# Feed-forward opening of a hybrid decoder trunk: three products of the two opened gate pairs in narrow form, and steps of the weight sums issued earlier

## The chip, the cores and the metric

The kernel runs on one core of a Trainium2 chip. A core has TensorE (PE, with its weight loads shown as PEld), VectorE (DVE), ScalarE (ACT), GpSimd (POOL) and SyncE (SP), which run side by side, each through its own queue in order, and 16 DMA engines that serve the queues of SP, ACT and POOL. Products are accumulated in PSUM, in banks of 128 x 512 float32. The metric is the device time of one execution in microseconds.

## The reference

Two decoder layers over 512 tokens of width 1024, in float32: the first mixes tokens by a gated short convolution, the second by sliding-window attention with sinks. Each is followed by the same feed-forward, with 2816 hidden channels, which is where the change lies:

```python
def swiglu(h, w_gate_up, w_down):
    g, u = jnp.split(h @ w_gate_up, 2, axis=-1)
    return (jax.nn.silu(g) * u) @ w_down

for l in range(DEPTH):
    ...
    ff = swiglu(rmsnorm(h, ffn_pre_norm[l]), ffn_w_gate_up[l], ffn_w_down[l])
    h = h + rmsnorm(ff, ffn_post_norm[l])
```

## The kernel before

**Precision.** Every operand is split into a high part (rounded by ScalarE, L504) and a low part (the rest, by VectorE, L505). A product is three matmuls: high by low, high by high, low by high (`mm3`, L209 to L212).

**Seven products.** The hidden channels are taken in 22 blocks of 128. The first two (PLAIN) are computed directly, as four plain tiles (`plain_job`, L1411; gate and up of each). The other 20 make ten pairs of blocks q = 0 to 9. For a pair, weights and tokens are cut into halves and the product is formed by a scheme of seven products instead of eight, numbered 1 to 7 (`gate_jobs`, L1218). Each product multiplies one sum of weight blocks with one sum of token blocks (`factors`), for e = 0 and 1 (gate and up) and four steps k. The results share PSUM: chain X takes products 1, 6, 7, 4 one on top of the other, Z takes 5 (and 3), Y takes 2. After each product `take` (L1243) adds the state of the chain to tiles in SBUF: `st`, `u` and `gr`, whose halves are g0 and g1. Because 6, 7 and 4 go on in the bank that the takes read, the matmuls of the next product of X wait for the take of the last one.

**Broad and narrow.** A broad chain (L1310 to L1316) has two banks, one for each e. A matmul 512 wide multiplies the high weights with high and low tokens side by side, so the two halves of a bank hold two parts of one sum, and a second matmul 256 wide adds the low weights. The take must add both halves of both banks: four operations on 128 x 256. A narrow chain (L1318 to L1321) has one bank: its halves are e = 0 and 1, and each k takes three matmuls of 256. One operation on 128 x 512 adds all of it. Here X is broad for all pairs, Z also from q = 3 on.

**Opened pairs.** For q = 0 and 1 (OPENED) products 1 and 2 are computed earlier, in narrow form, while the layer before ends (`Opening`, L1196). What is left are 6, 5, 7, 3, 4, with takes of their own (`early`, L1252 to L1267).

**Order.** A feed-forward is one list of jobs (`in_line`, L509): four plain tiles; five products of pair 0; five of pair 1; seven of pair 2; eleven jobs of the first down product (accumulated by L676); pair 3 and so on. When job j has run, job j + 3 (LINE_LEAD) is prepared: L504 and L505 split its weights, sometimes after L492 has added two weight tiles. Then one of the late parts of an earlier pair is run (L616 to L628). PE, VectorE, ScalarE and POOL keep this written order. Weights come through seven raw tiles on SP's queue (L471), each fetched when one is free.

**Sums of weights.** Other sums of weight blocks are made in HBM by POOL's DMAs, some of them accumulating (L575). `sum_on` (L595) first issues whatever is still left in a list, then puts the next step of each sum in progress on it. After every job, a few of the list are issued, each waiting for the split of the weights three jobs on (L539); behind a plain tile that has no such split they do not wait. The names at which a step is taken are in a table (BEGIN); "o1" and "0f0" (in layer 1 "1f0") are taken after the first plain tile, "0f1" (or "1f1") after the second.

Of the kernel before, what the change touches and what calls it, by code (L numbers as in the profile page):

```python
# [26 lines left out]
OPENED = 2  # L27
# [58 lines left out]
def yoco_kernel(  # L86
# [389 lines left out]
    class Job:  # L476
# [10 lines left out]
        def add(self):  # L487
            if callable(self.make):
                self.make()
            elif self.make:  # L490
                raw = self.raws[0].tile
                nc.vector.tensor_tensor(out=raw, in0=raw, in1=self.raws[1].tile, op=ALU.add)  # L492
# [92 lines left out]
    for l in range(2):  # L585
# [3 lines left out]
        for rd, (f0, f1) in enumerate(ROUNDS[:-1]):  # L589
            k = slice(f0 // 2, f1 // 2)  # L590
# [4 lines left out]
    def sum_on(at, behind=None):  # L595

        issue(len(issues), behind)
        if at in BEGIN:
            summing.append(sums_of[BEGIN[at]])
        for x in summing:  # L600
            x.step()
        summing[:] = [x for x in summing if x.steps]
# [169 lines left out]
    for k in range(KT):  # L772
# [11 lines left out]
        for n in range(9):  # L784
            i, t = (n % 3, n // 3) if k == 0 else (n // 3, n % 3)
            n = 3 * k + t
# [45 lines left out]
    both = []  # L832
# [342 lines left out]
    def ffn(l, before, ahead, gain, gpres, following):  # L1175
# [42 lines left out]
        def gate_jobs(q, factors, out, to, then):  # L1218

            sums = sums_of[f"g{l}{q}"]
            a21, a22, a11, a12 = (Raw(b) for b in sums.blocks)
            s1, s3, *rest = (Raw(b) for b in sums.sums)
            raws = {1: [a11], 2: [a12], 5: [s1], 7: [s3], 4: [a22]}
            if rest:
                raws[6], raws[3] = ([r] for r in rest)
            else:
                raws[6], raws[3] = [a11, s1], [a12, a11]
            five = q >= FIVE  # L1230
            broad = "XZ" if five else "X"
            chain = {1: "X", 6: "X", 7: "X", 4: "X", 5: "Z", 3: "V" if five else "Z", 2: "Y"}
            pools = {"X": ps_mm, "Y": ps_pt, "V": ps_pt, "Z": ps_sc}
            if q == 0:

                pools = {"X": ps_sc, "Y": ps_pt, "V": ps_pt, "Z": ps_mm}
            banks, kept = {}, []
            early = opened_pairs[q] if q < OPENED else None

            def tiles(a):  # L1240
                return a.rearrange("p (e c) -> p e c", e=2)

            def take(p):  # L1243
                x, y, z, v = (banks.get(c) for c in "XYZV")
                st, u, gr = kept[:3]
                g0, g1 = (gr.rearrange("p (e h c) -> p e h c", e=2, h=2)[:, :, h]
                          for h in range(2))

                def add(out, a, b):
                    nc.vector.tensor_tensor(out=out, in0=a, in1=b, op=ALU.add)  # L1250

                if early and p == 6:  # L1252
                    both = slot("st")
                    kept.append(both)
                    for e in range(2):
                        c = slice(e * 256, (e + 1) * 256)
                        add(both[:, c], x[e][:, :256], st[:, c])
                        add(both[:, c], x[e][:, 256:], both[:, c])
                elif early and p == 5:
                    add(u, z, st)  # L1260
                elif early and p == 3:
                    add(g1, tiles(z), tiles(kept[3]))
                elif early and p == 4:
                    for e in range(2):
                        c = slice(e * 256, (e + 1) * 256)
                        add(st[:, c], x[e][:, :256], st[:, c])
                        add(st[:, c], x[e][:, 256:], st[:, c])  # L1267
                elif p == 2:
                    add(g0, tiles(y), tiles(st))
                elif p == 5:  # L1270
                    if not five:
                        nc.scalar.activation(u, z, AF.Copy)
                        return
                    for e in range(2):
                        ue = u[:, e * 256 : (e + 1) * 256]
                        nc.scalar.activation(ue, z[e][:, :256], AF.Copy)
                        add(ue, z[e][:, 256:], ue)
                    add(st, u, st)
                elif p == 3:
                    add(g1, tiles(v if five else z), tiles(st))  # L1280
                else:
                    for e in range(2):
                        a, b = x[e][:, :256], x[e][:, 256:]
                        ste, ue = (v[:, e * 256 : (e + 1) * 256] for v in (st, u))
                        if p == 7:
                            add(ue, a, ue)
                            add(ue, b, ue)
                            continue
                        nc.scalar.activation(ste, a, AF.Copy)  # L1289
                        add(ste, b, ste)  # L1290
                if p == 4:
                    for g, m in ((g0, st), (g1, u)):
                        nc.vector.scalar_tensor_tensor(out=g, in0=tiles(m), scalar=-1.0, in1=g,
                                                       op0=ALU.mult, op1=ALU.mult)

            def run(p):
                def products(job):
                    if not kept:
                        kept.extend([early.st, slot("st"), early.gr] if early
                                    else [slot("st"), slot("st"), wide("gr")])  # L1300
                    whi, wlo = job.w
                    c = chain[p]
                    opened = c not in banks
                    if opened:
                        banks[c] = ([bank("g" + c.lower(), pools[c]) for _ in range(2)]
                                    if c in broad else bank("g" + c.lower(), pools[c]))
                    steps = [(e, k, slice(e * S + k * P, e * S + (k + 1) * P))
                             for e in range(2) for k in range(4)]
                    kw = {"skip_group_check": True}
                    if c in broad:  # L1310
                        for e, k, kk in steps:
                            nc.tensor.matmul(banks[c][e], whi[:, kk], factors[p][k][2],  # L1312
                                             start=opened and k == 0, stop=False, **kw)
                        for e, k, kk in steps:
                            nc.tensor.matmul(banks[c][e][:, :256], wlo[:, kk], factors[p][k][0],  # L1315
                                             start=False, stop=k == 3 and p in (4, 5), **kw)  # L1316
                    else:
                        for e, k, kk in steps:  # L1318
                            mm3(banks[c][:, e * 256 : (e + 1) * 256], whi[:, kk], wlo[:, kk],
                                *factors[p][k][:2], opened and e == k == 0,  # L1320
                                e == 1 and k == 3 and p in (2, 3), **kw)  # L1321
                    take(p)
                return products

            def gate():
                nc.scalar.activation(kept[2], kept[2], AF.Silu)  # L1326

            def end():
                late = out(kept[2], to)
                then()  # L1330
                return late

            return [Job(raws[p], run(p), {3: gate, 4: end}.get(p), len(raws[p]) > 1)
                    for p in (1, 2, 6, 5, 7, 3, 4)[2 if early else 0 :]]
# [41 lines left out]
        with tc.manual_schedule(engines=ALL):  # L1376
# [34 lines left out]
            def plain_job(n):  # L1411
                def run(job):
                    pss.append(bank("pgu", ps_mm))
                    project(pss[n], ahead.ready[2 * OPENED + n], xs)

                def then():
                    if n == 0:
                        if l == 0:
                            sum_on("o1")
                        sum_on(f"{l}f0")  # L1420
                    if n == 1:
                        sum_on(f"{l}f1")
                    return gate_pair(*pss[n - 1 :]) if n % 2 else None

                return Job([], run, then)
# [5 lines left out]
            for rd, (f0, f1) in enumerate(ROUNDS):  # L1431
                last = rd == len(ROUNDS) - 1
                for f in range(max(f0, PLAIN), f1, 2):
                    q = (f - PLAIN) // 2
# [10 lines left out]
            n = f1 - f0  # L1445
# [6 lines left out]
            for at, job in zip(LAST, closing):  # L1452
                job.slots = True
                jobs.insert(len(jobs) - at, job)
            in_line(jobs, late)
            if l == 1:
                nc.gpsimd.drain()
# [281 lines left out]
    early = [Early(u) for u in range(2 * NB)]  # L1739
    at = []  # L1740

    with tc.manual_schedule(engines=ALL):
# [20 lines left out]
        for hf in range(2):  # L1763
            c = slice(hf * 256, (hf + 1) * 256)
# [63 lines left out]
    with tc.manual_schedule(engines=ALL):  # L1828
        sum_on("a0")
        for i in range(KT + 2):  # L1830
# [9 lines left out]
            for c in order.split():  # L1840
# [23 lines left out]
                op, n = c[0], [int(d) for d in c[1:].rstrip("-")]  # L1864
                t = i - late
                if op == "g":

                    u = 2 * (t - EARLY - 1) + n[0]
# [128 lines left out]
```

## Time and profile before

| | us |
|---|---|
| median of 3 runs (lowest, highest) | 1018.8 (1018.78, 1019.55) |
| the profiled execution | 1019.24 |
| its span, first to last instruction | 1017.5 |
| PE busy | 999.8 |
| VectorE busy | 914.6 |
| ScalarE busy | 603.1 |
| POOL busy | 184.5 |

All times below count from the start of the span. Layer 0's opened pairs run from 211 to 243, layer 1's from 711 to 743.

A timeline row gives start, duration, engine, line, operation, tiles (out<-in), shape and how many such instructions were merged; in brackets, how long the engine stood idle before it and what ended that. Merged rows span all their instructions. Matmuls overlap, so PE's pace is read from start to start, not from durations. A row of waits gives total, number and longest. A row by stretches gives the window, its length, the busy time of PE, PEld, DVE, ACT and POOL (with instructions), then the granted TensorE clock as a share of full speed, the share of DMA time in use, and GB/s.

### The profile page before, as it was taken

What the parts mean: (1) busy time and instruction counts of PE and PEld (TensorE: products, weight loads), DVE (VectorE), ACT (ScalarE), POOL (GpSimd) and SP (SyncE); (2) the same over time, 40 slices, a digit from 0 to 9 for tenths busy, and PEclk for the clock granted to TensorE, in tenths of its full rate; (3) what the DMA queues carried; (4) which work ended last, traced back from release to release, by engine and by line L of the source; (5) the groups of instructions that cost most, each with busy time, mean ns of one, the idle gap of its engine ahead of it and who ended that gap; (6) DMA issues with size and microseconds to landing.
All of it is one profiled execution on the core that took longest, in us unless ns stands there. A gap on an engine that the chain in (4) does not pass through costs nothing. (4 is left out here: it accounts for less than half of the span.)

```text
span 1017.5 us, 16125 instructions
## 1 busy us (share of the span) xinstructions
PE 999.8 (98%) x5848; PEld 879.5 (86%) x5848; DVE 914.6 (90%) x1572; ACT 603.1 (59%) x1085; POOL 184.5 (18%) x250
## 2 busy tenths in 40 slices
PE   9999999998999999999999999999999999999997
PEld 7899888988889898898898888898888888989986
DVE  7899877899789999999878998878997999999996
ACT  8445545754656465566485788778446664645641
POOL 0211022112101011000022756420211010110001
PEclk9999999999999999999999999999999999999999
DMA  9886987678969789769504889965999576979742
GB/s 339 269 246 205 336 260 275 222 234 248 328 238 284 257 285 307 240 216 341 203 1 134 219 242 254 284 230 142 343 299 322 171 246 223 290 277 276 241 166 83
DMA packets 68447, 248.69 MB, mean 244 GB/s; under 512 B 8080, under 2 KB 8848, under 8 KB 56592
## 3 DMA queue, kind: packets, MB, share of 16 engines
q1 hardware_dynamic: 53200, 150.24, 39.7%
q0 software_dynamic: 14592, 96.48, 37.0%
q8 instruction: 46, 0.75, 0.3%
q10 hardware_dynamic: 576, 0.95, 0.2%
q14 instruction: 33, 0.27, 0.1%
HBM read 241.34 MB, written 102.76 MB: 338 GB/s over the span
## 5 line engine op out<-in xcount | busy, mean ns | idle before, releaser
L505 DVE TENSOR_TENSOR wlo<-raw,whi 128x1024 fp32r<-128x1024 f32 (+1 forms) x227 | 274.2, 1213 | 26.1 <-ACT whi L504 26.0
L504 ACT ACTIVATE whi<-raw 128x1024 fp32r<-128x1024 f32 (+1 forms) x227 | 234.8, 1050 | 103.8 <-DVE raw L492 59.1
L1312 PE MATMUL gx<-xt,whi 128*128 128x512 f32 x480 | 122.5, 398 | 6.9 <-DVE st L1250 6.9
L1312 PEld LDWEIGHTS gx<-xt,whi 128*128 128x128 f32 x480 | 87.3, 191 | 24.0 <-ACT whi L504 4.7
L575 POOL DMA_DIRECT2D hsum<-in_w_gb_dram x96 | 63.5, 722 | 156.5 <-ACT whi L504 109.9
L575 POOL DMA_DIRECT2D hsum<-hsum x32 | 25.3, 790 | 355.7 <-ACT whi L504 296.0
L1250 DVE TENSOR_TENSOR st<-gx,st 128x256 f32<-128x256 f32 x208 | 81.2, 418 | 4.7 <-PE gx L1315 2.0
L1315 PEld LDWEIGHTS gx<-xt,wlo 128*128 128x128 f32 x480 | 65.6, 191 | 4.8
L1315 PE MATMUL gx<-xt,wlo 128*128 128x256 f32 x480 | 66.9, 282 | 0.0
L1289 ACT ACTIVATE st<-gx 128x256 f32<-128x256 f32 x96 | 34.7, 380 | 50.6 <-PE gx L1315 41.6
L1326 ACT ACTIVATE gr<-gr 128x1024 f32<-128x1024 f32 x20 | 21.2, 1062 | 61.2 <-DVE gr L1250 61.2
L210 PE MATMUL px<-wlo,ahi 128*128 128x512 f32 x120 | 46.8, 390 | 1.5 <-DVE mix L676 1.5
L212 PE MATMUL px<-whi,alo 128*128 128x512 f32 x120 | 46.7, 389 | 0.0
L211 PE MATMUL px<-whi,ahi 128*128 128x512 f32 x120 | 46.7, 389 | 0.0
L575 POOL DMA_DIRECT2D hsum<-in_w_dn_dram x48 | 31.9, 765 | 80.3 <-ACT whi L504 64.2
L210 PE MATMUL gy<-xlo,whi 128*128 128x256 f32 x144 | 40.8, 283 | 0.0
L211 PE MATMUL gy<-xhi,whi 128*128 128x256 f32 x144 | 40.8, 283 | 0.0
L212 PE MATMUL gy<-xhi,wlo 128*128 128x256 f32 x144 | 40.7, 283 | 0.0
L676 DVE TENSOR_TENSOR mix<-mix,px 128x512 f32<-128x512 f32 x54 | 34.7, 679 | 1.5 <-PE px L212 1.5
L320 POOL TENSOR_TENSOR ur<-uv,mhalf 128x1 f32<-128x1 f32 x15 | 13.9, 928 | 113.7 <-DVE uv L315 113.6
L492 DVE TENSOR_TENSOR raw<-raw,raw 128x1024 f32<-128x1024 f32 x28 | 34.1, 1219 | 0.1
L442 ACT ACTIVATE whi<-raw 128x1024 fp32r<-128x1024 f32 x18 | 19.3, 1082 | 23.6 <-DMA raw<-in_w_gb_dram 7.9
(367 smaller groups left out, 3062.4 us busy)
## 6 DMA issues: line engine op xcount, KB each, us to landing
hsum<-in_w_gb_dram POOLq DMA_DIRECT2D x96, 512.0 KB, 7.9
raw<-hsum SPq DMA_DIRECT2D x88, 512.0 KB, 7.6
raw<-in_w_gb_dram SPq DMA_DIRECT2D x64, 512.0 KB, 6.7
hsum<-in_w_dn_dram POOLq DMA_DIRECT2D x36, 512.0 KB, 8.2
raw<-in_w_dn_dram SPq DMA_DIRECT2D x32, 512.0 KB, 6.6
hsum<-hsum POOLq DMA_DIRECT2D x28, 512.0 KB, 6.1
hsum<-in_w_dn_dram POOLq DMA_DIRECT2D x12, 768.0 KB, 13.6
raw<-in_w_in_dram SPq DMA_DIRECT2D x13, 512.0 KB, 6.9
```

Of the source, the lines that this page charges most:

```text
L210: nc.tensor.matmul(out, whi, xlo, start=start, stop=False, **kw)
L211: nc.tensor.matmul(out, whi, xhi, start=False, stop=False, **kw)
L212: nc.tensor.matmul(out, wlo, xhi, start=False, stop=stop, **kw)
L492: nc.vector.tensor_tensor(out=raw, in0=raw, in1=self.raws[1].tile, op=ALU.add)
L504: self.begun = nc.scalar.activation(hi[:, :n], raw, AF.Copy)
L505: nc.vector.tensor_tensor(out=lo[:, :n], in0=raw, in1=hi[:, :n].bitcast(F32), op=ALU.subtract)
L575: nc.gpsimd.dma_start(dst, src, max_dma_last_dim=4 * 4 * S, **kw))
L676: nc.vector.tensor_tensor(out=m, in0=m, in1=banks[bs][r], op=ALU.subtract if half else ALU.add)
L1250: nc.vector.tensor_tensor(out=out, in0=a, in1=b, op=ALU.add)
L1289: nc.scalar.activation(ste, a, AF.Copy)
L1312: nc.tensor.matmul(banks[c][e], whi[:, kk], factors[p][k][2], start=opened and k == 0, stop=False, **kw)
L1315: nc.tensor.matmul(banks[c][e][:, :256], wlo[:, kk], factors[p][k][0], start=False, stop=k == 3 and p in (4, 5), **kw)
```

## The change

Three things. For the opened pairs no chain is broad any more: products 6, 7 and 4 go narrow into one bank, as 5 and 3 already do. Their takes add the bank as a whole, one operation instead of four. And the calls of `sum_on` move: those for "o1" and "0f0" (or "1f0") from behind the first plain tile to ahead of the whole list of jobs, and the one for "0f1" (or "1f1") from behind the second plain tile to behind the first. What is computed stays the same but for the order of additions.

```diff
             five = q >= FIVE
-            broad = "XZ" if five else "X"
+            broad = "XZ" if five else "" if q < OPENED else "X"
...
                 if early and p == 6:
                     both = slot("st")
                     kept.append(both)
-                    for e in range(2):
-                        c = slice(e * 256, (e + 1) * 256)
-                        add(both[:, c], x[e][:, :256], st[:, c])
-                        add(both[:, c], x[e][:, 256:], both[:, c])
+                    add(both, x, st)
...
                 elif early and p == 4:
-                    for e in range(2):
-                        c = slice(e * 256, (e + 1) * 256)
-                        add(st[:, c], x[e][:, :256], st[:, c])
-                        add(st[:, c], x[e][:, 256:], st[:, c])
+                    add(st, x, st)
+                elif early and p == 7:
+                    add(u, x, u)
...
                             mm3(banks[c][:, e * 256 : (e + 1) * 256], whi[:, kk], wlo[:, kk],
                                 *factors[p][k][:2], opened and e == k == 0,
-                                e == 1 and k == 3 and p in (2, 3), **kw)
+                                e == 1 and k == 3 and p in ((4, 3) if early else (2, 3)),
+                                **kw)
...
                 def then():
                     if n == 0:
-                        if l == 0:
-                            sum_on("o1")
-                        sum_on(f"{l}f0")
-                    if n == 1:
                         sum_on(f"{l}f1")
...
+            if l == 0:
+                sum_on("o1")
+            sum_on(f"{l}f0")
             in_line(jobs, late)
```

## The prediction

> **What bounds the kernel now.** I read the page first, then the waits of TensorE, then the timelines around each wait, then the busy table by stretches.
>
> ```profile
> span 1017.5 us, 16125 instructions
> ...
> PE 999.8 (98%) x5848; PEld 879.5 (86%) x5848; DVE 914.6 (90%) x1572; ACT 603.1 (59%) x1085; POOL 184.5 (18%) x250
> ```
>
> TensorE is the bound almost everywhere, so a change is worth what it takes out of PE's few breaks, less what it adds to PE's own work. PE's waits, where PE was the one that waited:
>
> ```profile
> PE gx L1312 <- DVE st L1250: 6.9, 4, 2.2
> PE px L210 <- DVE mix L676: 1.5, 1, 1.5
> ```
>
> The first row is the X chain waiting for VectorE's adds at L1250, four times. PE's timeline in layer 0:
>
> ```profile
> 211.00 1.98 PE L1312 MATMUL gx<-xt,whi 128*128 128x512 f32 x8
> ...
> 213.76 0.28 PE L210 MATMUL gz<-xt,whi 128*128 128x256 f32 x1
> ...
> 216.65 2.00 PE L1312 MATMUL gx<-xt,whi 128*128 128x512 f32 x8
> ...
> 230.66 0.28 PE L212 MATMUL gz<-xt,wlo 128*128 128x256 f32 x1
> 233.11 3.65 PE L1312 MATMUL gx<-xt,whi 128*128 128x512 f32 x8 [2.17 <-DVE st L1250]
> ...
> 248.77 0.28 PE L212 MATMUL gy<-xhi,wlo 128*128 128x256 f32 x1
> 249.71 2.11 PE L1312 MATMUL gx<-xt,whi 128*128 128x512 f32 x8 [0.66 <-DVE st L1250]
> ```
>
> A 256-wide matmul starts every 0.12 us (213.76 to 216.65 holds 24). So the next start after 230.66 was due at 230.78 and came at 233.11: 2.33 us lost. The eight matmuls behind it took 3.65 us where those at 211.00 took 1.98: 1.67 more. At 249.71 another 0.82 is lost, and 0.11 in the group. Layer 0 loses 4.9 us. The same products in layer 1:
>
> ```profile
> 730.70 0.28 PE L212 MATMUL gz<-xt,wlo 128*128 128x256 f32 x1
> 733.14 2.08 PE L1312 MATMUL gx<-xt,whi 128*128 128x512 f32 x8 [2.17 <-DVE st L1250]
> ...
> 747.56 0.28 PE L212 MATMUL gy<-xhi,wlo 128*128 128x256 f32 x1
> 749.74 1.43 PE L1312 MATMUL gx<-xt,whi 128*128 128x512 f32 x5 [1.90 <-DVE st L1250]
> ```
>
> From 733.14 to 749.74 is 16.60 us, as from 233.11 to 249.71: the stage lasts the same in both layers, and only the breaks sit elsewhere (no slow group here, but 2.06 us at 749.74). VectorE sets this stage's length, as its own queue shows:
>
> ```profile
> 213.49 1.68 DVE L1250 TENSOR_TENSOR st<-gx,st 128x256 f32<-128x256 f32 x4 [0.98 <-PE gx L1315]
> ...
> 216.85 0.69 DVE L1250 TENSOR_TENSOR st<-gz,st 128x512 f32<-128x512 f32 x1 [0.22 <-PE gz L212]
> ...
> 226.24 1.67 DVE L1250 TENSOR_TENSOR st<-gx,st 128x256 f32<-128x256 f32 x4
> 228.01 1.29 DVE L1293 SCALAR_TENSOR_TENSOR gr<-st,gr 128x512 f32<-128x512 f32 x2
> 229.22 1.22 DVE L505 TENSOR_TENSOR wlo<-raw,whi 128x1024 fp32r<-128x1024 f32 x1
> 230.35 1.22 DVE L492 TENSOR_TENSOR raw<-raw,raw 128x1024 f32<-128x1024 f32 x1
> 231.49 0.68 DVE L628 TENSOR_TENSOR alo<-s,ahi 128x512 fp32r<-128x512 f32 x1
> 232.09 1.66 DVE L1250 TENSOR_TENSOR st<-gx,st 128x256 f32<-128x256 f32 x4
> ```
>
> From 216.85 on it has no idle time. The take of pair 1's sixth product could have begun at 228.0, when PE had closed that product (the 24 matmuls behind it end with the row at 230.66, so they began 2.75 us before), but VectorE came to it at 232.09; PE's seventh product waits for it because it accumulates into the same bank.
>
> **The change part by part.** *Takes.* Four adds of 256 (1.68) become one of 512 (0.69, the row at 216.85, same operands): 0.99 us less VectorE, for three takes in two pairs in two layers, 11.9 us in all, 5.9 a layer.
>
> *Products.* Eight 512-wide and eight 256-wide matmuls (211.00 to 213.76, 2.76 us) become 24 of 256 (2.89 us): 0.13 more PE each, on the path, 0.8 a layer, 1.6 in all. [...]
>
> *Waits.* With one bank per product VectorE may start only after the last of the 24 matmuls, not after the half. Also wlo is wanted with the third matmul instead of the ninth, 1.6 us sooner; it is made three products ahead, so 8 us of PE work cover it.
>
> *Ledger of layer 0*, from 211.00, in VectorE's unchanged order. Products end every 2.89 us; I add 0.3 for a matmul to finish. First take 214.1; behind it come the same steps, and the second and third of these takes at 220.6 and 225.6 (there it waits for PE). Then from the rows 228.01 to 232.09 the steps L1293, L505, L492 and L628, 1.21 + 1.13 + 1.14 + 0.60 us, put the take of pair 1's sixth product at 230.4 and its end at 231.1. PE wants its bank at 231.2: no break, but with 0.1 us to spare. On to pair 2: its sixth product starts at 245.5 instead of 249.71, 4.2 us earlier, and its take is ready at 245.4. That equals 4.9 lost less 0.8 added. Layer 1 has the same order and length, so 4.2 there as well.
>
> *What is late next: the loads in layer 0.* DMA share by stretches (the last two numbers: share, GB/s; the number before is the granted clock):
>
> ```profile
> 225.00:230.00 5.00, 5.00 (x37) 4.67 (x36) 4.83 (x9) 2.15 (x3) 0.00 (x0) 1.00 0.36 124
> 230.00:235.00 5.00, 2.83 (x13) 2.29 (x13) 4.93 (x9) 3.31 (x5) 1.96 (x3) 0.82 0.67 198
> 235.00:240.00 5.00, 5.00 (x34) 4.63 (x33) 4.93 (x9) 1.52 (x2) 1.49 (x3) 0.84 0.96 184
> ...
> 285.00:290.00 5.00, 3.83 (x17) 2.83 (x16) 3.28 (x6) 3.98 (x6) 0.00 (x0) 1.00 1.02 410
> ...
> 730.00:735.00 5.00, 2.83 (x17) 2.36 (x16) 4.93 (x9) 3.28 (x5) 1.93 (x3) 1.00 1.01 421
> ```
>
> All eleven stretches from 235 to 290 are full. Their start is set by POOL's batch of sums, and their end reaches PE:
>
> ```profile
> 233.04 0.80 POOL L575 DMA_DIRECT2D hsum<-hsum  x1 [18.54 <-ACT whi L504]
> ```
>
> ```profile
> 285.60 1.06 ACT L504 ACTIVATE whi<-raw 128x1024 fp32r<-128x1024 f32 x1 [4.18 <-DMA raw<-hsum]
> ```
>
> ```profile
> 289.57 1.28 DVE L676 TENSOR_TENSOR mix<-mix,px 128x512 f32<-128x512 f32 x2
> ```
>
> ```profile
> 288.45 0.39 PE L212 MATMUL py<-whi,alo 128*128 128x512 f32 x1
> 290.30 0.50 PE L210 MATMUL px<-wlo,ahi 128*128 128x512 f32 x1 [1.47 <-DVE mix L676]
> ```
>
> A load lands at 285.5, ScalarE splits it, VectorE's queue stands behind that split until it adds px at 289.57, and PE starts at 290.30. The batch at 233.04 waits for a split that follows the L492 at 230.35; in the ledger that L492 starts at 228.6, 1.75 us earlier. Full engines move the same bytes in the same time, so the load lands 1.8 us earlier, not 4.2, and PE restarts at 288.5. PE itself arrives at 284.5 (288.68 less 4.2) and now stands for 4 us. Bounds of that shift: 0 (bytes reordered against this load) and 5.8 (4.2, and the 1.6 us break gone, if the queue only looked full). I take 1.8, as the share rows are nearest.
>
> *The clock.* The group at 233.11 ran at half speed (clock 0.82 in that stretch, 1.67 us lost) after a break of 2.33; the equal break before 733.14 cost nothing (clock 1.00), nor did 2.06 at 749.74 or 1.6 at 290.30. One of two breaks of 2.3 dropped the clock; I take it that 4 us does, at 1.6 us. So layer 0 nets 1.8 - 1.6 = 0.2.
>
> *Layer 1's loads* have room: there the load of the same product is split without a DMA wait.
>
> ```profile
> 781.35 1.05 ACT L504 ACTIVATE whi<-raw 128x1024 fp32r<-128x1024 f32 x1
> ```
>
> I keep 4.2, bounds 2 (if loads bind there by half) and 5.
>
> *The moved steps.* POOL's queue in layer 0, and its first row of this stage in layer 1:
>
> ```profile
> 183.14 1.65 POOL L575 DMA_DIRECT2D hsum<-in_w_gb_dram  x2
> ...
> 206.95 1.62 POOL L575 DMA_DIRECT2D hsum<-in_w_dn_dram  x2 [20.15 <-ACT whi L504]
> 212.70 0.78 POOL L575 DMA_DIRECT2D hsum<-hsum  x1 [4.12 <-ACT a L617]
> 213.21 1.30 POOL L575 DMA_DIRECT2D hsum<-in_w_gb_dram  x2
> ```
>
> ```profile
> 706.98 0.77 POOL L575 DMA_DIRECT2D hsum<-hsum  x1 [22.14 <-ACT whi L504]
> ```
>
> Those from 183.14 on have nothing before them that moves, so they stay. The two at 206.95 are left over one plain tile earlier, where the third job on has no split to pace them: they go out once their copies have landed. The three at 212.70 and 213.21 follow the split of one job sooner. In layer 1 the row at 706.98 and the two copies behind it likewise lose their pace, and the steps of "f1" come a job sooner. Nothing but more such DMAs stands behind them on POOL's queue, and on SP's they pass loads that are fetched three jobs and more ahead. It empties the engines a little before 226, where they run out of work anyway (0.36), and it lightens layer 1's full stretch; the batch at 233.04 is put on the list after pair 0, as before. I take 0, bounds -0.5 (room for loads in layer 1) and +0.5 (in the way of a load).
>
> **Sum.** 4.2 + 0.2 = 4.4 us off. The profiled execution took 1019.24 us with its span of 1017.5, 0.4 above the median 1018.8; all terms are differences, so they come off the median: **1014.4**.
>
> **Rivals.** *No drop of the clock* in layer 0: 4.2 + 1.8 off, 1012.8. For it: 733.14 after 2.3 us; against it: 233.11, and a longer break. [...]
>
> *The loads follow*: the SP loads are asked for 4 us earlier too, and if they come so, each layer keeps 4.2 and the break at 290.30 goes: 8.4 + 1.6 off, 1008.8. Against it stand eleven full stretches.
>
> *Slower: the loads take everything, twice.* If no load lands earlier in either layer, PE gains nothing up to the down products, stands 4 us in each, and restarts slow in each: 2 x 1.6, 1022.0. It decides where ScalarE in layer 1 waits over 4 us for a load; the row at 781.35, without a wait, speaks against it.
>
> *It does nothing*: if VectorE's order and not its amount of work held PE, the freed time becomes idle time and PE pays 1.6: 1020.4. VectorE's unbroken queue speaks against it.
>
> **How the numbers follow.** Forecast 45%, no drop 28%, loads follow 14%, does nothing 7%, slower 6%. The first two, with the shift of the load a microsecond either way, span 1011.8 to 1016. The range adds half of "loads follow" below: 1009.8 to 1016.4. About 0.2% (2 us) is what a measurement of this kernel can tell from no change: faster 0.86, same 0.08, slower 0.06.
>
> **What would show it.** L1250 on gx with 512 elements three times a pair at 0.69; 24 matmuls in 2.9 us for X; no break before the seventh product of pair 1 nor the sixth of pair 2; pair 2's sixth product 4.2 us earlier after its layer's start; in layer 0 a longer wait of ScalarE for a load near 284 and of PE for px near 288, with a granted clock under 1 behind it. A break left at pair 1's seventh product would mean that the ledger's 0.1 us was too thin; px on time near 284.5 that the loads were not the limit.

## The result and the profile after

| | before | after |
|---|---|---|
| median of 7 runs (lowest, highest), us | 1018.8 (1017.79, 1019.55) | 1013.91 (1012.56, 1015.71) |
| ratio, 95% interval | | 0.9954 (0.9942 to 0.9966) |
| the profiled execution, us | 1019.24 | 1014.07 |

The kernel became 4.9 us faster; 1014.4 was forecast. First the page of the kernel after:

```profile
span 1012.3 us, 16275 instructions
...
PE 1000.0 (99%) x5944; PEld 884.5 (87%) x5944; DVE 904.8 (89%) x1536; ACT 602.9 (60%) x1085; POOL 184.0 (18%) x250
```

TensorE is as busy as it was (999.8 before), in a span 5.2 us shorter: what went is its standing still. Its waits (total, number, longest):

```profile
PE px L210 <- DVE mix L676: 2.5, 1, 2.5
...
PE px L210 <- ACT mix L674: 0.5, 1, 0.5
```

The row "gx <- DVE st L1250" (6.9 us) is gone. The wait for px has grown from 1.5 to 2.5 us, and a second wait in the same down product is new. TensorE's timeline after (narrow matmuls of X now run through L210 to L212; L1312 has become L1308):

```profile
211.32 0.28 PE L210 MATMUL gx<-xt,whi 128*128 128x256 f32 x1
...
214.19 0.28 PE L210 MATMUL gz<-xt,whi 128*128 128x256 f32 x1
...
231.35 0.28 PE L212 MATMUL gz<-xt,wlo 128*128 128x256 f32 x1
231.62 0.36 PE L210 MATMUL gx<-xt,whi 128*128 128x256 f32 x1
...
246.00 2.00 PE L1308 MATMUL gx<-xt,whi 128*128 128x512 f32 x8
...
268.10 0.39 PE L212 MATMUL pz<-whi,alo 128*128 128x512 f32 x1
268.96 0.50 PE L210 MATMUL px<-wlo,ahi 128*128 128x512 f32 x1 [0.47 <-ACT mix L674]
...
285.18 0.39 PE L212 MATMUL py<-whi,alo 128*128 128x512 f32 x1
288.05 0.79 PE L210 MATMUL px<-wlo,ahi 128*128 128x512 f32 x1 [2.48 <-DVE mix L676]
288.64 0.63 PE L211 MATMUL px<-whi,ahi 128*128 128x512 f32 x1
289.07 0.63 PE L212 MATMUL px<-whi,alo 128*128 128x512 f32 x1
...
293.67 1.98 PE L1308 MATMUL gx<-xhl,whi 128*128 128x512 f32 x8
...
710.16 0.28 PE L210 MATMUL gx<-xt,whi 128*128 128x256 f32 x1
...
787.58 1.98 PE L1308 MATMUL gx<-xhl,whi 128*128 128x512 f32 x8
```

Read start to start, the seventh product of pair 1 (231.62) comes 0.27 us after the matmul ahead of it, so it is 0.15 us late instead of 2.33. Pair 2's sixth product starts at 246.00 without a wait. Then come the two waits, 0.63 and 2.64 us beyond the usual 0.23 from start to start of a 512-wide matmul, and behind the second the matmuls start every 0.43 us until 291.

The stage from the first matmul of the opened pairs to the first of pair 3 holds the whole difference. In the timeline of the kernel before the three rows that bound it, beside the one at 211.00, are:

```profile
294.53 1.75 PE L1312 MATMUL gx<-xhl,whi 128*128 128x512 f32 x7
...
711.03 1.98 PE L1312 MATMUL gx<-xt,whi 128*128 128x512 f32 x8
...
792.78 1.98 PE L1312 MATMUL gx<-xhl,whi 128*128 128x512 f32 x8
```

Layer 0's stage went from 83.53 to 82.35 us, layer 1's from 81.75 to 77.42. Between the stages lie 416.50 us before and 416.49 after, behind the second 224.7 in both, and the first begins 0.32 later: 1.18 + 4.33 - 0.32 = 5.2, the difference of the spans. So layer 1 gave nearly four times what layer 0 did, for the same edit.

VectorE after, at the place where pair 1's take was late:

```profile
214.39 0.69 DVE L1250 TENSOR_TENSOR st<-gx,st 128x512 f32<-128x512 f32 x1 [1.57 <-PE gx L212]
...
229.05 1.22 DVE L492 TENSOR_TENSOR raw<-raw,raw 128x1024 f32<-128x1024 f32 x1
230.19 0.69 DVE L628 TENSOR_TENSOR alo<-s,ahi 128x512 fp32r<-128x512 f32 x1
230.79 0.68 DVE L1250 TENSOR_TENSOR st<-gx,st 128x512 f32<-128x512 f32 x1
```

The take begins at 230.79 instead of 232.09 and lasts 0.68 instead of 1.66, in the same order of steps. Then ScalarE's timeline and the busy table by stretches of the kernel after:

```profile
265.99 1.06 ACT L504 ACTIVATE whi<-raw 128x1024 fp32r<-128x1024 f32 x1 [3.14 <-DMA raw<-hsum]
...
283.35 1.06 ACT L504 ACTIVATE whi<-raw 128x1024 fp32r<-128x1024 f32 x1 [5.20 <-DMA raw<-hsum]
```

```profile
220.00:225.00 5.00, 5.00 (x44) 5.00 (x44) 4.97 (x9) 3.46 (x4) 0.00 (x0) 1.00 0.37 108
225.00:230.00 5.00, 5.00 (x44) 5.00 (x43) 4.75 (x7) 1.59 (x3) 0.00 (x0) 1.00 0.32 105
...
285.00:290.00 5.00, 2.52 (x8) 1.71 (x7) 4.97 (x10) 2.87 (x4) 0.00 (x0) 0.76 1.03 415
```

Both new waits have a load behind them: ScalarE stands 3.14 us and later 5.20 us for a raw tile, and what TensorE needs next is queued behind the split. From 285 to 290 the DMA engines are full (1.03) and the clock is at 0.76; from 220 to 230 the engines are two thirds empty.

### The profile page after: what moved, and what is told of

Read it like the earlier page. It is cut to its first block, busy times and chain, and to the rows that moved or that the text cites. A ratio compares the mean times of both kernels' runs of the same rounds, so it can differ in the third digit from the quotient of the medians.

```text
span 1012.3 us, 16275 instructions
## 1 busy us (share of the span) xinstructions
PE 1000.0 (99%) x5944; PEld 884.5 (87%) x5944; DVE 904.8 (89%) x1536; ACT 602.9 (60%) x1085; POOL 184.0 (18%) x250
## 5 line engine op out<-in xcount | busy, mean ns | idle before, releaser
L1308 PE MATMUL gx<-xt,whi 128*128 128x512 f32 x384 | 96.4, 393 | 0.0
L1308 PEld LDWEIGHTS gx<-xt,whi 128*128 128x128 f32 x384 | 69.1, 189 | 12.4
L1250 DVE TENSOR_TENSOR st<-gx,st 128x256 f32<-128x256 f32 (+1 forms) x172 | 70.5, 439 | 5.3 <-PE gx L212 3.1
L1311 PEld LDWEIGHTS gx<-xt,wlo 128*128 128x128 f32 x384 | 52.4, 191 | 3.7
L1311 PE MATMUL gx<-xt,wlo 128*128 128x256 f32 x384 | 53.6, 283 | 0.0
L210 PE MATMUL px<-wlo,ahi 128*128 128x512 f32 x120 | 47.6, 397 | 2.9 <-DVE mix L676 2.5
L212 PE MATMUL px<-whi,alo 128*128 128x512 f32 x120 | 47.3, 394 | 0.0
L210 PE MATMUL gy<-xlo,whi 128*128 128x256 f32 x144 | 40.8, 283 | 0.0
L212 PE MATMUL gy<-xhi,wlo 128*128 128x256 f32 x144 | 40.8, 283 | 0.0
```

Of the source, the lines that this page charges most:

```text
L210: nc.tensor.matmul(out, whi, xlo, start=start, stop=False, **kw)
L212: nc.tensor.matmul(out, wlo, xhi, start=False, stop=stop, **kw)
```

## The experiments

The theory after this result: three limits lie over each stage, TensorE's own work, VectorE's takes, and in layer 0 the loads behind GpSimd's sums. The change lowers the second; in layer 1 the first takes over, in layer 0 the third. The rivals were the moved sum steps as the source of the gain, and the clock as what eats layer 0's share. The ratios below are taken over all runs of a set and can differ a little from the quotient of the two medians.

### The moved sum steps alone

```diff
                     if n == 0:
-                        if l == 0:
-                            sum_on("o1")
-                        sum_on(f"{l}f0")
-                    if n == 1:
                         sum_on(f"{l}f1")
...
+            if l == 0:
+                sum_on("o1")
+            sum_on(f"{l}f0")
```

> The moved steps of the weight sums alone; products and takes as in the kernel before. Theory (VectorE's amount of work in the opening held TensorE, the steps give nothing): 1018.8 us, within 0.5, and TensorE's breaks of 2.3 us at pair 1's seventh product and of 0.8 to 2.1 us at pair 2's sixth stay. Rival (the steps bring a good part of the 4.9 us): 1017 us or less.

Measured: 1019.95 us against 1019.24 for the kernel before, ratio 1.0003 (0.9989 to 1.0017). Its waits of TensorE:

```profile
PE gx L1312 <- DVE st L1250: 5.7, 4, 2.2
...
PE px L210 <- DVE mix L676: 0.4, 1, 0.4
```

The four waits of X are still there. The median lies above the theory's 1018.8, but so does that of the kernel before in this set. The wait for px shrank by 1.1 us, because the split ahead of it began at 283.88 instead of 285.60; in the time nothing shows. By the interval the steps alone bring 1.1 us at most, so the gain of 4.9 is not theirs.

### The narrow products and takes without the moved steps

```diff
-            broad = "XZ" if five else "X"
+            broad = "XZ" if five else "" if q < OPENED else "X"
...
-                    for e in range(2):
-                        c = slice(e * 256, (e + 1) * 256)
-                        add(both[:, c], x[e][:, :256], st[:, c])
-                        add(both[:, c], x[e][:, 256:], both[:, c])
+                    add(both, x, st)
```

> The narrow products and single takes alone; the steps of the sums stay where they were before. Theory: 1013.9 us, within 0.7, as the whole change. Rival (the steps bring a good part): 1015.5 us or more, with ScalarE waiting for loads in layer 1.

Measured: 1015.15 us against 1019.24, ratio 0.9967 (0.9956 to 0.9977). The median lies between the theory (1014.6 at most) and the rival (1015.5 at least), so the time decides for neither. The interval overlaps the whole change's from 0.9956 to 0.9966, and a microsecond for the moved steps on top is possible but not settled. Of the rival's sign there is one wait: ScalarE stands 2.70 us for a load in layer 1 (until 754.59), but TensorE does not, and layer 1's stage lasts as long as in the kernel after. TensorE's timeline at px:

```profile
284.79 0.39 PE L212 MATMUL py<-whi,alo 128*128 128x512 f32 x1
288.09 0.50 PE L210 MATMUL px<-wlo,ahi 128*128 128x512 f32 x1 [2.91 <-DVE mix L676]
288.42 0.39 PE L211 MATMUL px<-whi,ahi 128*128 128x512 f32 x1
288.65 0.40 PE L212 MATMUL px<-whi,alo 128*128 128x512 f32 x1
```

The break is longer than in the kernel after (3.07 us against 2.64), and still the matmuls behind it start every 0.23 us: here the clock did not drop, and layer 0's stage lasted 80.99 us. That prices the drop. Up to px the stage lasts 76.74 us here and 76.73 in the kernel after; from px to pair 3 it lasts 4.25 us here and 5.62 there, so the drop costs 1.4 us. The profiled execution took 1012.83 us, the fastest of this kernel's eight, so its trace shows what it is like without a drop and not a typical run.

### The whole change, with VectorE's freed time filled again

```diff
+                def again(a):
+                    for c in (slice(0, 256), slice(256, 512), slice(0, 256)):
+                        nc.vector.tensor_tensor(out=a[:, c], in0=a[:, c], in1=a[:, c], op=ALU.max)
...
                     add(both, x, st)
+                    again(both)
```

(and likewise behind the takes of products 7 and 4).

> The whole change, and behind each single take three operations of 256 on VectorE that change no value (the maximum of a tile with itself), so that VectorE has about its old amount of work. Theory (amount of work): the breaks at pair 1's seventh and pair 2's sixth product come back, 5 us a layer less what layer 0 loses to the loads anyway, and the narrow products cost 1.6 us on top: 1019 to 1020.5 us. Rival (the narrow form and its single bank free TensorE, not VectorE's time): 1014 to 1015 us without those breaks.

Measured: 1020.61 us against 1019.24, ratio 1.0016 (1.0006 to 1.0026). TensorE's waits:

```profile
PE gx L210 <- DVE st L1250: 4.7, 2, 2.3
PE gx L1315 <- DVE st L1250: 2.5, 2, 1.2
```

The breaks are back at the same two places in both layers. VectorE is busy for 916.7 us here, 2.1 more than in the kernel before, and the time is 0.1 us above the theory's range. It is VectorE's amount of work in the takes that held TensorE, not the number of banks.

### One layer at a time

In the first of these two kernels the opened pairs are narrow in layer 0 alone, in the second in layer 1 alone; the sum steps are moved in both. Against the kernel after:

```diff
-            broad = "XZ" if five else "" if q < OPENED else "X"
+            narrow = q < OPENED and l == 0
+            broad = "XZ" if five else "" if narrow else "X"
```

> Narrow products and single takes in layer 0 alone; the steps of the sums as after. Theory (layer 0 keeps only what its loads allow, 1.2 us by the two traces, 0.2 by the forecast's working): 1017.6 to 1018.6 us, with the break and the slow matmuls near 285. Rival (both layers give the same): 1016.4 us.

> Narrow products and single takes in layer 1 alone; the steps of the sums as after. Theory (layer 1 keeps all of the 4.2 us): 1014.5 us, within 0.6. Rival (both layers give the same): 1016.4 us.

Measured, against 1018.38 for the kernel before: layer 0 alone 1019.5 us, ratio 1.0004 (0.9993 to 1.0015); layer 1 alone 1014.22 us, ratio 0.9956 (0.9943 to 0.9969). Waits with layer 0 alone:

```profile
PE gx L1319 <- DVE st L1251: 2.8, 2, 2.2
PE px L210 <- DVE mix L676: 2.0, 1, 2.0
...
PE px L210 <- ACT mix L674: 0.9, 1, 0.9
```

X waits only in layer 1 now (2 times, not 4), and the two load-bound waits of layer 0 have taken the place of the others; behind the second the clock drops (at 289.28). Layer 1 alone came out as the theory had it. Layer 0 alone missed its 1017.6 to 1018.6 us: no gain can be measured. So all of the gain that can be measured is gained in layer 1.

### TensorE kept busy in the break of layer 0

```diff
+                    if l == 0 and first and parts == [(4, 0)]:
+                        idle = bank("idle", ps_sc)
+                        for _ in range(12):
+                            nc.tensor.matmul(idle[:, :P], ones, ones, start=True, stop=True)
```

> The whole change, and twelve matmuls of 128 columns into an unused bank ahead of layer 0's fourth down product, about 2.5 us of TensorE work in the break before px that reach no output. Theory (the slow matmuls come from TensorE's idle time): the break is filled, the matmuls behind it start every 0.23 us, 1.6 us less: 1012.3 us. Rival (the slow clock has another cause, or the loads set the time behind the break as well): slow matmuls stay, or they go and the time stays at 1013.9 us.

Measured: 1013.54 us against 1018.38, ratio 0.995 (0.9937 to 0.9963), no different from the change without the filling. TensorE's timeline (the twelve matmuls show as 24 instructions):

```profile
287.38 2.84 PE L1361 MATMUL idle<-ones 128*128 128x128 f32 x24
289.97 0.48 PE L210 MATMUL px<-wlo,ahi 128*128 128x512 f32 x1
290.29 0.40 PE L211 MATMUL px<-whi,ahi 128*128 128x512 f32 x1
```

The slow matmuls are gone, but in this execution two load-bound waits ahead of the filling (1.2 us at 269.86, 0.9 at 284.52) had already brought TensorE there 2 us later, and the filling runs on to 289.97, past the 288.05 at which px was ready in the kernel after. What the clock alone costs can't be read from this run; it is inconclusive, and the 1.4 us above come from the two traces compared there.

### The sums of layer 0 on the list one name earlier

```diff
-    "0f1": "g05", "0p0": "g06", "0p1": "d02", ...
+    "0f0": "g05", "0f1": "g06", "0p0": "d02", ...
```

> The whole change, and in layer 0 three sums begin one name earlier (the fifth gate sum at the first step of the feed-forward, the sixth at the next, the third down sum behind pair 0), in time when the DMA engines have room. Theory (layer 0's wait at the fourth down product is for a load that stands behind full DMA engines, and the slow clock follows from that wait): the load that lands at 283.2 comes 2 us or more earlier, the break of 2.6 us before px shrinks under 1 us, the slow matmuls behind it go: 1010 to 1011.5 us. Rival (the load is late for its own queue's sake, not for what POOL moves beside it): 1013.9 us, load at 283.

Measured: 1009.17 us (1009.11 to 1009.29 in 4 runs) against 1019.24, ratio 0.9903 (0.9889 to 0.9917). This beats both kernels, by 4.7 us the one after (1013.91, measured in another set of runs), and comes out under the theory's 1010 to 1011.5. Its ScalarE timeline and its busy table by stretches:

```profile
277.99 1.06 ACT L504 ACTIVATE whi<-raw 128x1024 fp32r<-128x1024 f32 x1 [0.61 <-DMA raw<-hsum]
```

```profile
220.00:225.00 5.00, 5.00 (x44) 5.00 (x44) 4.97 (x9) 3.48 (x4) 0.50 (x1) 1.00 1.03 420
225.00:230.00 5.00, 5.00 (x44) 5.00 (x43) 4.75 (x7) 1.58 (x3) 0.00 (x0) 1.00 0.98 394
...
285.00:290.00 5.00, 5.00 (x24) 4.14 (x23) 5.00 (x7) 2.92 (x5) 0.00 (x0) 1.00 0.10 40
```

The stretch that stood two thirds empty is now full, and in return the one at 285 is empty (0.10). The split that had waited 5.20 us and begun at 283.35 begins at 277.99. Neither of layer 0's waits is left, the smaller one at 268.96 included.

### The earlier list with the broad products

The same line of the table, on the kernel with the moved steps alone.

> The kernel before (broad X, four adds a take) with the moved sum steps and the earlier list of weight sums in layer 0 (g05, g06 and d02 each one name sooner). Theory (two limits in series in layer 0: VectorE's takes hold the opened pairs, and the load behind the batch of sums holds the down product; whichever is later counts): with the load out of the way the stage from the opened pairs to pair 3 lasts in layer 0 what it lasts in layer 1 in the broad form, 81.7 us, where it lasted 83.5 before and 82.5 with the moved steps alone; VectorE's breaks of about 2.3 us stay. Time about 1018.5 (1017.3 to 1019.3), 0.8 to 1.8 less than the moved steps alone. Rival (the earlier list is worth its 4.7 us by itself, whatever the form of the products): 1014 to 1015.5.

Measured: 1017.89 us against 1018.0, ratio 0.9995 (0.9986 to 1.0005). Its waits of TensorE:

```profile
PE gx L1312 <- DVE st L1250: 8.1, 4, 2.2
```

With the loads out of the way VectorE holds layer 0 as it holds layer 1: both stages last 81.74 us, as the theory had it (81.7). The list brings nothing that can be measured by itself, and 4.7 us behind the narrow form.

### The earlier list and the narrow form, with the sum steps where they were

The same line of the table, on the kernel with the narrow products and takes alone.

> Narrow products and takes with the earlier list of weight sums, but the calls of the sum steps where they stood before, behind the first and the second plain tile. Theory (the steps' place plays no part; what counts is when the sums behind the load of the down product are on the list): layer 0 without the break before px, 1009 to 1010.5, as with the moved steps. Rival (only the moved calls make the earlier list early enough, since a step is now taken a plain tile later): a break before px of 1 us and more is left, 1011.5 to 1014.

Measured: 1016.12 us against 1018.0, ratio 0.9977 (0.9965 to 0.9989). The theory falls here, and by more than its rival allowed; the break isn't at px either. TensorE's timeline and ScalarE's:

```profile
262.44 0.39 PE L212 MATMUL px<-whi,a 128*128 128x512 f32 x1
267.43 0.80 PE L210 MATMUL pz<-wlo,ahi 128*128 128x512 f32 x1 [4.61 <-DVE wlo L505]
```

```profile
265.06 1.06 ACT L504 ACTIVATE whi<-raw 128x1024 fp32r<-128x1024 f32 x1 [8.07 <-DMA raw<-hsum]
```

GpSimd's timelines tell why, first of this kernel, then of the one with the moved steps:

```profile
207.04 1.61 POOL L575 DMA_DIRECT2D hsum<-in_w_dn_dram  x2 [20.16 <-ACT whi L504]
...
220.59 2.78 POOL L575 DMA_DIRECT2D hsum<-in_w_gb_dram  x5 [1.51 <-DMA hsum<-in_w_gb_dram]
```

```profile
194.14 0.80 POOL L575 DMA_DIRECT2D hsum<-in_w_dn_dram  x1 [7.04 <-DMA hsum<-in_w_dn_dram]
196.36 0.79 POOL L575 DMA_DIRECT2D hsum<-in_w_dn_dram  x1 [1.42 <-DMA hsum<-in_w_dn_dram]
...
208.89 0.79 POOL L575 DMA_DIRECT2D hsum<-in_w_gb_dram  x1 [0.82 <-DMA hsum<-in_w_gb_dram]
```

With the old place of the calls, the two copies from in_w_dn_dram go out at 207.04 instead of 194.14 and 196.36, and the copies that were put on the list behind them pile up, five at 220.59. A raw tile asked for by SP at 234.84 then lands at 264.96, 30.1 us later; with the moved steps the same one is asked for at 235.05 and lands at 252.22. So the moved steps, worth nothing on the old list, carry the new one.

### All stages side by side

From the first matmul of the opened pairs to the first of pair 3, from each kernel's trace, in us. Each is one execution: the moved steps alone and narrow in layer 1 alone run the same code in layer 0, and their traces differ by 0.7 us there.

| kernel | layer 0 | layer 1 |
|---|---|---|
| before | 83.53 | 81.75 |
| moved steps alone | 82.47 | 81.75 |
| narrow, steps not moved | 80.99 | 77.41 |
| after | 82.35 | 77.42 |
| after, takes filled again | 82.96 | 82.93 |
| narrow in layer 0 alone | 82.51 | 81.74 |
| narrow in layer 1 alone | 81.76 | 77.42 |
| after, TensorE kept busy in the break | 82.56 | 77.42 |
| broad, earlier list | 81.74 | 81.74 |
| narrow, earlier list, steps not moved | 83.81 | 77.80 |
| narrow, earlier list | 77.41 | 77.41 |

Layer 1 has two values: 81.74 where VectorE's four adds hold it and 77.41 where TensorE's own work does (the filled takes hold it longer still, and one kernel loses 0.4 to short waits). Layer 0 reaches these values only where the loads allow it; the other kernels lie between 81 and 84 there, by the load and the clock.

## Why the prediction was right

**What bounds.** VectorE's amount of work set the opened pairs' length, as read from its queue: with its time filled again the breaks returned.

**Takes.** One add of 512 lasts 0.69 us, as forecast. In all, 48 adds of 0.418 us on average became 12 of 0.688, which is 11.8 us less where 11.9 was forecast. The busy time counts overlap once, and by it these adds fell by 10.6 us and VectorE by 9.8.

**Products.** From 211.32 to 214.19 are 2.87 us against 2.76: 0.11 each instead of 0.13.

**The ledger.** It had pair 1's take end 0.1 us before TensorE wants the bank; TensorE started 0.15 us late. Pair 2's sixth product starts 34.68 us after the opened pairs began instead of 38.71: 4.0 us earlier, where 4.2 was forecast. In layer 1 it starts 34.69 us after (744.85) instead of 38.71, again 4.0 earlier, and no load comes in the way. At the stage's end it is 4.33 us: two slow restarts of 0.11 us each, at 749.74 and 755.61 in the kernel before, went too, and the last 0.1 us is not traced. The term 4.2 was right to within 0.2, and the run with layer 1 alone shows it by itself.

**Layer 0's loads.** It was right that a load ends the wait and comes less early than TensorE. The reason for its 1.8 us was not borne out. The batch went out 1.3 us earlier (231.75), the split began 2.25 us earlier (283.35), and TensorE came to the break 3.27 us earlier (285.18 against 288.45): the load followed neither. With the moved steps alone the split began 1.72 us earlier though the batch went out 0.37 us later (233.41). Nor do full engines move the same bytes in the same time: the eleven full stretches of the kernel before (share 0.96 to 1.08) moved 184 to 416 GB/s. That the sums put on the engines before it set when the load lands is shown by the earlier list; why it was 2.25 us here stays open. So px restarted at 288.05 instead of 288.5, near the forecast without its reason. TensorE stood less at px (2.64 against 4 us): px was ready 0.45 us sooner than forecast, the stage had begun 0.32 us later, and TensorE had already stood 0.63 us at 268.96 for ScalarE, whose queue was behind a split that waited 3.14 us for another load: a wait that the prediction didn't have.

**The clock.** It dropped behind that break and cost 1.4 us, where 1.6 was forecast. But that was for a break of 4 us; behind the 2.64 that came, the drop was luck, since with 3.07 us of break and narrow products alone it did not come (the last section sets the breaks side by side).

**Layer 0's sum.** Forecast were 1.8 - 1.6 = 0.2 us. In the traces px restarts 2.57 us earlier, counted from the stage's start, and from px to pair 3 it takes 1.39 longer: 1.18 us. The timed runs with layer 0 alone give between 0.7 us of gain and 1.5 of loss. So the term stands within what can be measured, as a difference of two terms that were each a little off.

**The moved steps.** 0 was right for this change as far as 1.0003 (0.9989 to 1.0017) can tell. The reason given, that they empty the engines where these run out of work anyway, was half of it: the earlier list gains its 4.7 us only with them.

**The rivals.** "No drop of the clock" was priced at 1012.8, and the one profiled execution with narrow products and no drop took 1012.83: that kernel differs from the one after only in the place of the sum steps, and the median of 1013.91 lies between the rival and the forecast. "The loads follow" was priced at 1008.8; with the earlier list they do follow, and 1009.17 came out. "It does nothing" and "slower" have fallen: no load binds in layer 1, and the freed VectorE time became TensorE time. One sum of the range does not come out: 1014.4 with the load a microsecond later is 1015.4, not 1016, so the range was wider above than its reasons; the result did not need that.

## What to carry to other kernels

Where an edit repeats in two stages, read for each stage which limit comes next before adding the two gains: here one stage gave 4.3 us and the other nothing that could be measured until its loads were moved. A nearly empty stretch of the DMA engines ahead of a full one (here 0.37 and 0.32 from 220 to 230, ahead of 1.03 from 285 to 290) is the place to look for the next gain; here sums issued earlier filled it (1.03 and 0.98). An edit that measures nothing alone may be the one that another needs, so test the pairs.

## What was not expected of the hardware

The drop of the granted clock doesn't follow the length of the break alone. The same break of 2.33 us dropped it in layer 0 of the kernel before and not in layer 1, and 3.07 us (narrow, steps not moved) did not drop it. In the kernel before and in the one after the clock stood at 0.50 for 3.41 us, as these stretches of the busy table show:

```profile
233.20:236.61 3.41, 3.41 (x9) 2.67 (x10) 3.38 (x6) 2.26 (x4) 2.78 (x4) 0.50 1.00 243
```

```profile
287.64:291.05 3.41, 3.00 (x7) 2.42 (x8) 3.41 (x6) 0.97 (x2) 0.00 (x0) 0.50 0.96 384
```

Seven breaks, in order of their length, and what came behind them:

| break | TensorE stands, us | what came behind it |
|---|---|---|
| narrow in layer 0 alone, to 287.90 | 2.02 | 512-wide matmuls every 0.23 us, from 289.48 on every 0.43 |
| before, layer 0, to 233.11 | 2.17 | clock 0.50 from 233.20 on |
| before, layer 1, to 733.14 | 2.17 | clock 1.00 |
| after, takes filled again, to 234.43 | 2.34 | 256-wide matmuls every 0.12 us, from 235.94 on every 0.21 |
| after, layer 0, to 288.05 | 2.48 | clock 0.50 from 287.64 on |
| narrow, steps not moved, to 288.09 | 2.91 | clock 1.00 |
| narrow, earlier list, steps not moved, to 267.43 | 4.61 | clock 0.72 from 265 to 270, matmuls every 0.43 us |

The slow stretch began 0.41 us before TensorE's restart in the kernel after, 0.09 us behind it in the kernel before, and about 1.5 us behind it in the first and the fourth row. What decides is not shown by these runs. The one break of more than 4 us (4.61) dropped the clock, as the prediction took it that 4 us would; that is a single case. Nor did each drop cost time: in the kernel before, where VectorE held the stage, 233.11 to 249.71, with a drop (mean clock 0.90), and 733.14 to 749.74, without one (1.00), both last 16.60 us.

Kernels with such breaks also scatter from run to run, by 3.2 us after and 3.7 with narrow products alone, while the one without them scattered by 0.2 us over 4 runs. The clock explains this at most in part. Each run's mean clock is on record: in the kernel after the two fastest runs have the highest (1012.56 and 1013.17 at 0.998 and 0.999), but with narrow products alone 1012.83 and 1015.21 came at the same 0.998, and the kernel before took between 1017.63 and 1022.55 at the same 0.995. The rest of the scatter is open.

A load's time from issue to landing was 17.2 us with the earlier list and 30.1 us for the same tile with the steps not moved; the two kernels differ only in the place of the calls, and so in when GpSimd put its copies on the DMA engines.
